# A scan's hand-written order rewoven: block 2's preparation, the first merge and the second solve in one stretch

## The chip, the cores and the metric

The kernel runs on one core of one Trainium2 chip. The metric is the device time of one execution in microseconds. Three runs of the kernel before took 2351.26, 2352.57 and 2353.73 us; the median is 2352.57.

## The reference

The reference is one layer of an encoder: a half-step feed-forward network, then a mixer made of an attention group and a recurrent group side by side, then a second half-step network. All is in float32, with 1024 tokens of width 1024. The part that matters here is the recurrent group, eight heads of width 64, scanned forwards and backwards, and the output projection of the attention group, which fills gaps in the scan:

```python
def _rwkv7_step(state, inp):
    r, w, k, v, kk, kka = inp
    sa = jnp.einsum('dbhvk,dbhk->dbhv', state, kk)
    state = state * w[..., None, :] - sa[..., :, None] * kka[..., None, :] + v[..., :, None] * k[..., None, :]
    y = jnp.einsum('dbhvk,dbhk->dbhv', state, r)
    return state, y
...
        mix = jnp.concatenate([y_att, y_rwkv], axis=-1) @ w_out[l]
        h = h + _rmsnorm(mix, mix_post_g[l])
```

## The kernel before

The kernel does not step through the tokens. It cuts them into 16 chunks of 64, takes two chunks as a block (8 blocks, both directions at once), and turns the recurrence inside a chunk into matrix products and one triangular inverse. Each block passes through these parts, written as Python generators or closures, so that the order of their pieces can be written out by hand in `scan` (lines 1068 to 1224):

- **Loads and preparation** (`prep_loads`, `prep_parts`). Per direction: `exps` (two exponentials on ScalarE), `times` (five VectorE products, lines 861 to 869, and a ScalarE copy), `triangles` (32 TensorE matmuls in two pairs of halves, `lp`, line 876, each followed by `masks`, VectorE products with a triangle mask, line 878), `turns` (32 TensorE transposes, `bp`, line 888, and two ScalarE copies). `lp` and `bp` share three PSUM banks. `store` writes the diagonal 32 x 32 blocks to DRAM, from where the solve loads them regrouped as `X`.
- **Solve** (`solve_parts`): 31 steps of two VectorE instructions each (lines 936 and 938) that invert the 32 x 32 triangles, then a transpose (line 941). `go(solve, n)` issues n steps, and each mask is followed by one.
- **Merge** (`merge_parts`): three groups of small matmuls into one PSUM bank `pa` (lines 953, 959, 966) that join the 32 x 32 inverses to 64 x 64 ones, with ScalarE copies between them (954, 961, 962, 968). It needs the block's solve.
- **Chain** (`chain_parts`): fourteen pieces: two of ScalarE copies (line 1002), and then six for each of the two chunks: `xu` (line 1014) and its copy `xs`, the old state into `st`, `xu` again (line 1027) and its copies `uv`, a first `y`, `st` and a second `y` (line 999) with the copy `yb`, and the new state `sv` (VectorE, line 1049). Chunk follows chunk through `sv`: this is the sequential spine of the scan.
- **Attended tiles** (`attended_weights`, `attended_parts`): the attention group's output projection, 8 tiles of 128 tokens. The weights are first split in high and low halves (`woh` on ScalarE, `wol` on VectorE, lines 1298 and 1299). Each tile has six pieces: transposes `yq` of the loaded rows (line 1346) and the copy `yah`; `yal` (VectorE, line 1352); four of six `po` matmuls of 512 columns each (line 1325), two for each half of the output width. The second and fourth of these copy `po` out (`yao`, line 1360), and the fourth scales the next tile's rows (line 1337). `yq` and `po` share one PSUM bank, `eo`.

The framework gives each engine its own instruction queue. `in_order` chains all instructions of the scan on TensorE, VectorE and ScalarE in the order in which `scan` emits them, so that an instruction that waits holds everything emitted after it on its engine. Loads on SyncE's queue, GpSimd's work and instructions from outside the scan are placed by the framework's scheduler. The scan's prologue handles block 0 (solved earlier) together with the end of block 1's solve and the preparation of block 2; the loop `for m in range(1, NB - 2)` runs merge and chain of block m, the solve of block m + 1 and the preparation of block m + 2; two closing passes handle blocks 6 and 7. In the trace the copies of line 961 wait for the products of line 959, which write other partitions of the same PSUM bank.

Of the kernel before, what the change touches and what calls it, by code (L numbers as in the profile page):

```python
# [10 lines left out]
F32 = mybir.dt.float32  # L11
# [10 lines left out]
H, HD = 8, 64  # L22
# [141 lines left out]
class _Kernel:  # L164
# [660 lines left out]
    def prep_loads(self, n, d, p):  # L825
# [6 lines left out]
        ak = [p.tile([128, 4, TB], F32, name=nm, tag=nm, bufs=b) for nm, b in (("ka", 2), ("kd", 1))]  # L832
        for j in range(2):
            self.load(ak[j], self.ak_d[d][4 * j:4 * j + 4, :, ls].rearrange("a p t -> p a t"))
        x3 = p.tile([128, 2, 4, TB], F32, name="in2", tag="in2", bufs=1)
        self.load(x3.rearrange("p j a t -> p (j a) t"), self.rk_d[:, :, ts].rearrange("a p t -> p a t"))
        return cum, ak, x3

    def prep_parts(self, n, p, psum, big, loaded):
# [17 lines left out]
        def times(d):  # L857
            cum, ak, x3 = loaded.pop(d)
            x = {nm: x3[:, j, :, ::-1] if d else x3[:, j] for j, nm in enumerate(("r", "kk"))}
# [83 lines left out]
    def merge_parts(self, n, blk, p, psum):  # L943
# [10 lines left out]
        A.copy(tt[:, :, 32:64], pa)  # L954
        yield
# [4 lines left out]
        for lo, hi in lohi:  # L960
            A.copy(tt[lo, :, 0:32], pa[lo])
        A.copy(am, pa)
        yield
        for j in range(NI):
            for lo, hi in lohi:
                T.matmul(pa[lo, j, :], am[hi, j, :], tt[hi, j, 32:64], start=True, stop=True)  # L966
        for lo, hi in lohi:
            A.activation(tt[lo, :, 32:64], pa[lo], AF.Copy, scale=-1.0)
# [22 lines left out]
    def chain_parts(self, n, blk, c, psum):  # L991
# [13 lines left out]
        for i in range(BLK):  # L1005
            ch = n * BLK + i
            first = ch == 0
            uv = self.chain_values(ch, c)
            sv, nx = self.states(ch, c), self.states(ch + 1, c)
# [58 lines left out]
    def scan(self, blk, NB, sp, sc, eo, pm, pp, pc, pe, homes):  # L1068
# [32 lines left out]
        loads(2, 0)  # L1101
        parts(2)
        exps, times, triangles, turns, store = P.pop(2)
        go(solve, 5)
        times(0)
        loads(2, 1)
        go(solve, 4)
        masks(triangles(0, 0), solve)
        masks(triangles(0, 1), solve)
        exps(1)  # L1110
        turns(0)
        go(solve, 3)
        times(1)
        loads(3, 0)
        masks(triangles(1, 0), solve)
        masks(triangles(1, 1), solve)
        for _ in solve:
            pass
        store()

        merge, chain, solve = begin(0)
        weights = self.attended_weights(eo, W)
        go(weights)
        go(merge)
        turns(1)
# [4 lines left out]
        solving(2)  # L1130
        go(weights)
        solve = solves.pop(2)
        rs_a = self.rstd(eo, self.ss_a.rearrange("p a b -> p (a b)"), NT * H, 1.0 / HD, EPS)
        go(chain, 6)
        go(weights)
# [584 lines left out]
```

## Time and profile before

| What | us |
|---|---|
| median of three runs | 2352.57 |
| the profiled execution, its own time | 2355.06 |
| its span | 2353.3 |
| TensorE busy | 2198.4 |
| VectorE busy | 1774.3 |
| ScalarE busy | 1025.0 |
| first merge matmul to the last stretch's end in the scan (1273.6 to 1597.5) | 323.9 |

In the profile PE is TensorE, PEld its weight loads, DVE VectorE, ACT ScalarE, POOL GpSimd and SP SyncE; a q behind a name is the engine's queue for DMA issues. A row of the timeline gives the start, the length, the engine, the line in the kernel, the operation, what it writes and reads, the shape and how many such instructions it joins; brackets at its end give the idle time before it and what ended that. A matmul's length in a row is longer than its distance to the next one, because matmuls overlap in the array. A row of stretches gives the busy time of each engine between two times, and the TensorE clock that was granted, as a share of full speed.

### The profile page before, as it was taken

The numbers are of one execution on the slowest core, as the hardware profiler recorded it, in microseconds if no ns is written. First come the engines' busy times: TensorE is split into PE (matmuls) and PEld (weight loads), VectorE is DVE, ScalarE is ACT, GpSimd is POOL, SyncE is SP. The second block draws the span as 40 slices with busy tenths as digits, with TensorE's granted clock in tenths as the row PEclk, the third lists the DMA queues.
The fourth block names the chain that finished last, engine by engine and source line by source line (L and its number), as shares of the span: only waits on it lengthen the run. The fifth ranks groups of instructions, "written<-read, shape, count | busy, mean of one in ns | idle before, by whom it ended". The sixth has DMA issues, their size and how long they took to land. (4 is left out here: it accounts for less than half of the span.)

```text
span 2353.3 us, 41391 instructions
## 1 busy us (share of the span) xinstructions
PE 2198.4 (93%) x15556; PEld 1771.9 (75%) x15556; DVE 1774.3 (75%) x2893; ACT 1025.0 (44%) x1925; POOL 538.5 (23%) x673
## 2 busy tenths in 40 slices
PE   6999999999999998999996788879889999999998
PEld 5788888788877676787774667656678888887887
DVE  7999999865675344777776666746999999997566
ACT  5333333354676404666544454445542333335453
POOL 2344344400000011322211101122024343442000
PEclk9999999999999999999986888889989999999999
DMA  5354544576652515654377454536534544448665
GB/s 150 126 177 152 171 162 151 182 256 197 224 170 100 194 46 163 186 152 144 108 186 189 118 155 139 137 121 236 173 105 165 175 155 163 169 149 269 195 190 191
DMA packets 346700, 387.74 MB, mean 165 GB/s; under 512 B 73474, under 2 KB 249346, under 8 KB 346500
## 3 DMA queue, kind: packets, MB, share of 16 engines
q1 hardware_dynamic: 294928, 271.71, 38.1%
q0 software_dynamic: 31216, 100.73, 11.5%
q10 hardware_dynamic: 20356, 12.66, 1.8%
q8 instruction: 122, 2.00, 0.4%
q14 instruction: 78, 0.64, 0.1%
HBM read 258.06 MB, written 126.94 MB: 164 GB/s over the span
## 5 line engine op out<-in xcount | busy, mean ns | idle before, releaser
L81 PE MATMUL gu<-xh,wh 128*128 128x512 f32 x704 | 276.9, 393 | 4.6 <-ACT wh L186 4.5
L186 ACT ACTIVATE wh<-raw 128x512 fp32r<-128x512 f32 (+1 forms) x273 | 168.3, 627 | 249.5 <-PE gu L81 92.8
L81 PE MATMUL gu<-xl,wh 128*128 128x512 f32 x704 | 275.6, 391 | 0.0
L81 PE MATMUL gu<-xh,wl 128*128 128x512 f32 x704 | 275.5, 391 | 0.0
L187 DVE TENSOR_TENSOR wl<-raw,wh 128x512 fp32r<-128x512 f32 (+1 forms) x273 | 269.1, 989 | 3.4 <-ACT wh L186 2.6
L421 PE MATMUL pd<-gl,gwh 128*128 128x512 f32 x616 | 241.2, 391 | 3.1 <-DVE gl L187 3.1
L421 PE MATMUL pd<-gh,gwl 128*128 128x512 f32 x616 | 240.5, 390 | 0.2 <-DVE gwl L187 0.2
L421 PE MATMUL pd<-gh,gwh 128*128 128x512 f32 x616 | 239.9, 390 | 0.4 <-DVE row L86 0.4
L86 DVE TENSOR_TENSOR row<-gu,row 128x512 f32<-128x512 f32 x308 | 206.7, 683 | 23.1 <-PE gu L81 20.8
L187 DVE TENSOR_TENSOR gwl<-graw,gwh 128x512 fp32r<-128x512 f32 (+2 forms) x187 | 119.0, 644 | 124.8 <-ACT gwh L186 122.7
L116 POOL DMA_DIRECT2D d_hid<-row x154 | 85.1, 553 | 546.8 <-DVE row L114 526.7
L186 ACT ACTIVATE gwh<-graw 128x512 fp32r<-128x512 f32 (+2 forms) x187 | 102.9, 553 | 183.5 <-PE pd L421 150.5
L81 PEld LDWEIGHTS gu<-xh,wh 128*128 128x128 f32 x704 | 133.3, 189 | 33.5 <-ACT wh L186 5.6
L81 PEld LDWEIGHTS gu<-xh,wl 128*128 128x128 f32 x704 | 133.1, 189 | 28.0 <-DVE wl L187 0.2
L81 PEld LDWEIGHTS gu<-xl,wh 128*128 128x128 f32 x704 | 133.2, 189 | 27.4
L421 PEld LDWEIGHTS pd<-gl,gwh 128*128 128x128 f32 x616 | 116.2, 189 | 28.2 <-DVE gl L187 4.4
L421 PEld LDWEIGHTS pd<-gh,gwh 128*128 128x128 f32 x616 | 115.7, 188 | 25.4 <-DVE row L86 0.7
L421 PEld LDWEIGHTS pd<-gh,gwl 128*128 128x128 f32 x616 | 116.2, 189 | 24.8 <-DVE gwl L187 0.6
L187 DVE TENSOR_TENSOR gl<-raw,gh 128x512 fp32r<-128x512 f32 x160 | 113.3, 719 | 23.6 <-ACT gh L186 23.5
L94 ACT ACTIVATE row<-row 128x512 f32<-128x512 f32 x44 | 27.8, 633 | 214.3 <-DVE row L86 214.2
L186 ACT ACTIVATE gh<-raw 128x512 fp32r<-128x512 f32 x160 | 98.1, 621 | 42.1 <-DMA raw<-in_ffn_w_down_dram 24.4
L145 POOL TENSOR_TENSOR ws<-ws 128x512 f32<-128x512 f32 x88 | 114.8, 1305 | 1.2
(364 smaller groups left out, 5214.9 us busy)
## 6 DMA issues: line engine op xcount, KB each, us to landing
d_hid<-row POOLq DMA_DIRECT2D x154, 256.0 KB, 2.4
graw<-d_hid SPq DMA_DIRECT2D x132, 256.0 KB, 3.1
raw<-in_ffn_w_gate_dram SPq DMA_DIRECT2D x88, 256.0 KB, 3.1
raw<-in_ffn_w_up_dram SPq DMA_DIRECT2D x88, 256.0 KB, 3.5
ws<-in_ffn_w_down_dram SPq DMA_DIRECT2D x88, 256.0 KB, 4.1
d_ws<-ws POOLq DMA_DIRECT2D x88, 256.0 KB, 2.3
raw<-d_ws SPq DMA_DIRECT2D x88, 256.0 KB, 2.7
raw<-in_ffn_w_down_dram SPq DMA_DIRECT2D x66, 256.0 KB, 3.6
```

The source lines that it names most:

```text
L81: self.K.nc.tensor.matmul(ps, a[:, k, :], b[:, k, :], start=(k == 0 and i == 0), stop=(k == 3 and i == 2))
L86: add = lambda o, x: V.tensor_tensor(o, ps, x, op=OP.add)
L94: A.activation(y[:, 0], y[:, 0], AF.Silu)
L116: put = lambda n, y: G.dma_start(self.hid[n - 1, j // 2], y)
L145: G.tensor_tensor(o, a, b, op=OP.subtract)
L186: self.nc.scalar.activation(h, src, AF.Copy)
L187: (eng or self.nc.vector).tensor_tensor(l, src, h, op=OP.subtract)
L421: T.matmul(ps[x], a[:, ts], b, start=(m == 0 and k == 0), stop=(m == NM - 1 and k == 2))
```

## The change

The order in `scan` is written anew, and five helpers are adapted to it.

- The prologue loads both directions of block 2 at once (the second direction's `kd` and inputs into buffers of the `eo` pool that later hold split weights), and weaves block 2's preparation, the first merge and the solve of block 1 together; the chain's pieces, the weight splits and the solve of block 2 follow in a new order, and the prologue now ends with nine pieces of attended work issued instead of six.
- In the loop, `turns(0)` moves between the chunks of the chain, and `turns(1)` behind the first merge product of the next pass (`pend`). triangles(0, 0) stands between the second and third merge products. triangles(1, 0) moves into the second chunk. Each tile's two first `po` pieces stand in two places of the pass, the two others and the next tile's transposes at its end. The extra attended tile moves from m = 3 to m = 1.
- `merge_parts` copies line 961's parts before the second group of products, and gets one more yield before its last copies.
- The raw attended weights of k = 1 and 3 are loaded into the tiles `yat` and `yal`, so that two pairs are loaded at the start.
- The second half of each `po` (dh = 1) uses the merge's PSUM bank `mg` instead of `eo`.

```diff
@@ -822,19 +823,26 @@
         with self.tc.issue_after(last):
             return product().ins
 
-    def prep_loads(self, n, d, p):
+    def prep_loads(self, n, d, p, q=None):
 
         ls = slice(n * TB, (n + 1) * TB)
         b = n if d == 0 else NC_ // BLK - 1 - n
         ts = slice(b * TB, (b + 1) * TB)
         cum = p.tile([128, 4, TB], F32, name="th_w", tag="th_w", bufs=2)
         self.load(cum, self.lr_d["w"][d][:, :, ls].rearrange("a p t -> p a t"))
-        ak = [p.tile([128, 4, TB], F32, name=nm, tag=nm, bufs=b) for nm, b in (("ka", 2), ("kd", 1))]
+        ak = [p.tile([128, 4, TB], F32, name="ka", tag="ka", bufs=2),
+              q.tile([128, 4, TB], F32, name="kd", tag="woh", bufs=8) if q else
+              p.tile([128, 4, TB], F32, name="kd", tag="kd", bufs=1)]
         for j in range(2):
             self.load(ak[j], self.ak_d[d][4 * j:4 * j + 4, :, ls].rearrange("a p t -> p a t"))
+        if q:
+            x2 = [q.tile([128, 4, TB], F32, name="in1", tag="woh", bufs=8) for j in range(2)]
+            for j in range(2):
+                self.load(x2[j], self.rk_d[4 * j:4 * j + 4, :, ts].rearrange("a p t -> p a t"))
+            return cum, ak, x2
         x3 = p.tile([128, 2, 4, TB], F32, name="in2", tag="in2", bufs=1)
         self.load(x3.rearrange("p j a t -> p (j a) t"), self.rk_d[:, :, ts].rearrange("a p t -> p a t"))
-        return cum, ak, x3
+        return cum, ak, [x3[:, j] for j in range(2)]
 
     def prep_parts(self, n, p, psum, big, loaded):
 
@@ -855,8 +863,8 @@
             A.activation(flat(cum), flat(cum), AF.Exp, scale=-1.0)
 
         def times(d):
-            cum, ak, x3 = loaded.pop(d)
-            x = {nm: x3[:, j, :, ::-1] if d else x3[:, j] for j, nm in enumerate(("r", "kk"))}
+            cum, ak, x2 = loaded.pop(d)
+            x = {nm: x2[j][:, :, ::-1] if d else x2[j] for j, nm in enumerate(("r", "kk"))}
             ei = chunks(cum)
             V.tensor_copy(gc[:, d], e4[:, :, :, C])
             pt = blk["pr"][d] = big.tile([128, 4, BLK, 128], F32, name="pr", tag=f"pr{d}")
@@ -952,18 +960,19 @@
             for r in [r for lo, hi in lohi for r in (hi, lo)]:
                 T.matmul(pa[r, j, :], D[r, j, :], self.ident[r, r], start=True, stop=True)
         A.copy(tt[:, :, 32:64], pa)
+        for lo, hi in lohi:
+            A.copy(tt[lo, :, 0:32], pa[lo])
         yield
         for j in range(NI):
             d, i, pr = j // 8, j // 4 % 2, j % 4
             for par, (lo, hi) in enumerate(lohi):
                 T.matmul(pa[hi, j, :], lm[lo, par, d, i, pr, 32:64], D[lo, j, :], start=True, stop=True)
-        for lo, hi in lohi:
-            A.copy(tt[lo, :, 0:32], pa[lo])
         A.copy(am, pa)
         yield
         for j in range(NI):
             for lo, hi in lohi:
                 T.matmul(pa[lo, j, :], am[hi, j, :], tt[hi, j, 32:64], start=True, stop=True)
+        yield
         for lo, hi in lohi:
             A.activation(tt[lo, :, 32:64], pa[lo], AF.Copy, scale=-1.0)
 
@@ -1005,8 +1014,8 @@
         for i in range(BLK):
             ch = n * BLK + i
             first = ch == 0
-            uv = self.chain_values(ch, c)
-            sv, nx = self.states(ch, c), self.states(ch + 1, c)
+            sv = self.states(ch, c)
+            uv, nx = self.chain_values(ch, c), self.states(ch + 1, c)
             bank = lambda nm: psum.tile([128, 2, 4, 64], F32, name=nm, tag=nm, bufs=1)
             xu, st, y = bank("xu"), bank("st"), bank("y")
             for d, pr, par in heads:
@@ -1099,56 +1108,64 @@
         solve = self.solve_parts(1, sp, blk[1])
         go(solve, 9)
         loads(2, 0)
+        loaded[2][1] = self.prep_loads(2, 1, sp, eo)
         parts(2)
         exps, times, triangles, turns, store = P.pop(2)
+        weights = self.attended_weights(eo, W)
+        go(weights)
         go(solve, 5)
         times(0)
-        loads(2, 1)
-        go(solve, 4)
-        masks(triangles(0, 0), solve)
-        masks(triangles(0, 1), solve)
         exps(1)
+        loads(3, 0)
+        mask = triangles(0, 0)
+        go(solve, 2)
+        masks(mask, solve)
+        mask = triangles(0, 1)
+        times(1)
+        masks(mask, solve)
         turns(0)
-        go(solve, 3)
-        times(1)
-        loads(3, 0)
-        masks(triangles(1, 0), solve)
-        masks(triangles(1, 1), solve)
-        for _ in solve:
-            pass
+        merge, chain, _ = begin(0)
+        go(merge)
+        mask = triangles(1, 0)
+        go(solve, 2)
+        masks(mask, solve)
+        go(merge)
+        mask = triangles(1, 1)
+        go(solve, 2)
+        masks(mask, solve)
         store()
-
-        merge, chain, solve = begin(0)
-        weights = self.attended_weights(eo, W)
-        go(weights)
-        go(merge)
-        turns(1)
+        solving(2)
         go(merge)
         go(chain)
         go(merge)
         go(chain)
-        solving(2)
+        for _ in solve:
+            pass
+        turns(1)
+
         go(weights)
+        go(chain, 5)
         solve = solves.pop(2)
-        rs_a = self.rstd(eo, self.ss_a.rearrange("p a b -> p (a b)"), NT * H, 1.0 / HD, EPS)
-        go(chain, 6)
-        go(weights)
-        go(solve, 4)
-        go(chain, 5)
-        go(solve, 8)
         go(weights)
         go(chain)
+        go(chain, 3)
+        go(solve, 6)
+        go(chain, 2)
+        go(weights)
+        go(solve, 6)
+        go(chain)
+        rs_a = self.rstd(eo, self.ss_a.rearrange("p a b -> p (a b)"), NT * H, 1.0 / HD, EPS)
+        go(weights)
+        rest = self.attended_parts(eo, sc, pe, pm, list(range(NT)), W, rs_a)
+        go(rest, 2)
+        parts(3)
+        go(solve, 3)
+        go(rest, 5)
         go(solve, 2)
-        rest = self.attended_parts(eo, sc, pe, list(range(NT)), W, rs_a)
-        go(weights)
-        go(rest)
-        parts(3)
-        go(rest)
-        go(solve, 3)
-        go(rest, 4)
-        go(solve, 3)
+        go(rest, 2)
         solves[2] = solve
         blk.pop(0)
+        pend = lambda: None
 
         for m in range(1, NB - 2):
             merge, chain, solve = begin(m)
@@ -1157,13 +1174,15 @@
             times(0)
             go(merge)
             loads(k, 1)
+            pend()
+            go(merge)
+            mask = triangles(0, 0)
+            go(solve, 4)
             go(merge)
             go(chain)
-            mask = triangles(0, 0)
-            go(solve, 4)
-            masks(mask, solve)
             go(merge)
             go(chain)
+            masks(mask, solve)
             masks(triangles(0, 1), solve)
             exps(1)
             go(rest)
@@ -1171,44 +1190,54 @@
             times(1)
             loads(k + 1, 0)
             go(chain, 4)
+            go(solve, 2)
+            turns(0)
+            go(chain)
             go(solve, 3)
+            go(chain, 3)
             mask = triangles(1, 0)
             go(chain)
+            masks(mask, solve)
+            go(chain)
             go(solve, 3)
-            masks(mask, solve)
-            go(chain, 5)
-            go(solve, 4)
             go(chain)
+            go(rest)
             mask = triangles(1, 1)
-            go(solve, 2)
+            go(solve, 3)
             masks(mask, solve)
             store()
             solving(k)
+            go(rest, 3)
+            go(solve, 4)
             go(rest)
-            turns(0)
-            turns(1)
-            go(solve, 2)
-            go(rest, 4)
+            if m == 1:
+                go(solve, 2)
+                go(rest, 5)
+                go(rest)
             parts(k + 1)
             for _ in solve:
                 pass
-            if m == 3:
-                go(rest, 6)
+            pend = functools.partial(turns, 1)
             blk.pop(m)
 
         merge, chain, solve = begin(NB - 2)
         go(merge)
-        go(solve, 6)
+        pend()
+        go(solve, 5)
+        go(merge)
+        go(solve, 2)
         go(merge)
         go(chain)
-        go(solve, 3)
         go(merge)
+        go(chain)
+        go(solve, 4)
         go(rest)
         go(chain)
         go(solve, 2)
-        go(chain, 5)
-        go(solve, 13)
+        go(chain, 4)
+        go(solve, 10)
         go(chain)
+        go(rest)
         go(chain, 5)
         for _ in solve:
             pass
@@ -1216,7 +1245,7 @@
         for _ in rest:
             pass
         merge, chain, solve = begin(NB - 1)
-        go(merge, 2)
+        go(merge, 3)
         go(chain)
         go(merge)
         for _ in chain:
@@ -1285,19 +1314,30 @@
 
     def attended_weights(self, p, W):
 
+        raw = {}
+
+        def load(k):
+            for dh in range(2):
+                tag = ("wor", ("yat", "yal")[dh])[k % 2]
+                raw[k, dh] = p.tile([128, 512], F32, name="wor", tag=tag, bufs=1 if k % 2 else 2)
+                self.load(raw[k, dh], self.io["w_out"][0][k * 128:(k + 1) * 128, dh * 512:(dh + 1) * 512])
+
+        load(0)
+        load(1)
+        yield
         for k in range(4):
             hl = []
             for dh in range(2):
-                r = p.tile([128, 512], F32, name="wor", tag="wor", bufs=2)
-                self.load(r, self.io["w_out"][0][k * 128:(k + 1) * 128, dh * 512:(dh + 1) * 512])
                 h = p.tile([128, 512], F32R, name="woh", tag="woh", bufs=8)
                 l = p.tile([128, 512], F32R, name="wol", tag="wol", bufs=8)
-                hl.append((h, l, r))
-            yield
-            for h, l, r in hl:
+                r = raw.pop((k, dh))
                 self.nc.scalar.activation(h, r, AF.Copy, scale=self.aog[:, k:k + 1])
                 self.nc.vector.scalar_tensor_tensor(l, r, self.aog[:, k:k + 1], h, op0=OP.mult, op1=OP.subtract)
-            W.append([(h, l) for h, l, r in hl])
+                hl.append((h, l))
+            W.append(hl)
+            if k < 2:
+                load(k + 2)
+            yield
 
     def out_weights(self, p, k0, gain=None, raw=None):
 
@@ -1324,7 +1364,7 @@
             for j, (a, w) in enumerate(((xh, h), (xh, l), (xl, h))):
                 self.nc.tensor.matmul(ps, a[:, k, ts], w, start=(k == 0 and j == 0), stop=(k == 3 and j == 2))
 
-    def attended_parts(self, p, c, psum, tiles, W, rs_a):
+    def attended_parts(self, p, c, psum, other, tiles, W, rs_a):
 
         nc, V, A, T = self.nc, self.nc.vector, self.nc.scalar, self.nc.tensor
 
@@ -1352,7 +1392,7 @@
             V.tensor_tensor(l, q, h, op=OP.subtract)
             yield
             for dh in range(2):
-                ps = psum.tile([128, 512], F32, name="po", tag="eo")
+                ps = (psum, other)[dh].tile([128, 512], F32, name="po", tag=("eo", "mg")[dh])
                 for part in range(2):
                     self.out_products(ps, W, dh, h, l, slice(0, 128), range(2 * part, 2 * part + 2))
                     if part:
```

More of the change, by code (lines that the diff above doesn't have):

```diff
@@ L1 @@
+import functools
 import math
```

## The prediction

> **What bounds the kernel now.** I read the page first, for where the time is and which engine carries it.
>
> ```profile
> span 2353.3 us, 41391 instructions
> PE 2198.4 (93%) x15556; PEld 1771.9 (75%) x15556; DVE 1774.3 (75%) x2893; ACT 1025.0 (44%) x1925; POOL 538.5 (23%) x673
> ```
>
> TensorE is busy 93% of the span, so only stretches where it waits can be shortened by an order. The change touches the scan alone. I cut the scan at the first merge matmul of each block (line 953) and asked for the busy time of each stretch.
>
> ```profile
> core 0: us, PE busy (x) PEld busy (x) DVE busy (x) ACT busy (x) POOL busy (x), PEclk, DMA share, GB/s
> 1246.30:1273.60 27.30, 13.83 (x97) 11.06 (x96) 21.02 (x55) 6.90 (x12) 7.60 (x13) 0.64 0.92 242
> 1273.60:1325.00 51.40, 29.47 (x592) 25.05 (x591) 29.44 (x82) 22.77 (x38) 5.63 (x11) 0.63 0.45 122
> 1325.00:1360.30 35.30, 31.06 (x721) 25.69 (x721) 15.42 (x35) 17.77 (x32) 5.64 (x11) 0.95 0.52 132
> 1360.30:1400.80 40.50, 33.70 (x809) 28.13 (x810) 30.80 (x89) 18.57 (x34) 5.64 (x11) 0.92 0.56 158
> 1400.80:1451.40 50.60, 42.41 (x680) 34.13 (x669) 34.59 (x101) 20.86 (x37) 5.64 (x11) 0.83 0.55 151
> 1451.40:1491.40 40.00, 34.81 (x718) 28.96 (x717) 26.03 (x75) 17.74 (x32) 5.65 (x11) 0.83 0.45 122
> 1491.40:1529.60 38.20, 32.23 (x721) 26.51 (x720) 29.89 (x86) 17.34 (x32) 4.77 (x8) 0.91 0.48 132
> 1529.60:1568.30 38.70, 27.96 (x627) 23.02 (x626) 20.88 (x69) 12.56 (x23) 9.37 (x14) 0.87 0.47 141
> 1568.30:1597.50 29.20, 24.81 (x614) 19.19 (x613) 9.78 (x16) 19.85 (x35) 4.72 (x6) 0.88 0.25 77
> ```
>
> The first two rows, the end of block 2's preparation and the pass of block 0, take 78.7 us with TensorE busy 43.3 of them at a clock of 0.63: there is most to win. The next five are the loop (m = 1 to 5; m = 3 holds an extra attended tile). In them TensorE waits 4 to 8 us each and VectorE is already busy 26 to 31 us of about 40. The last two are the two closing blocks. The chain of waits says what ends TensorE's idle time; these are from 1223 to 1598 us, as total, times, longest.
>
> ```profile
> PE yq L1346 <- DVE yat L1337: 10.0, 1, 10.0
> PE po L1325 <- DVE yal L1352: 9.5, 7, 2.3
> PE pa L959 <- issue: 8.2, 4, 3.5
> PE pa L966 <- ACT am L962: 8.0, 6, 1.9
> PE bp L888 <- DVE lm L878: 7.0, 10, 1.4
> PE po L1325 <- ACT yao L1360: 5.4, 8, 0.7
> PE pa L959 <- ACT tt L954: 5.3, 7, 0.9
> ```
>
> The waits of `bp`, `po` and `pa` are about 5 us per block, and the change names a filler or a second bank for every one of them except "issue". The question is whether VectorE lets that be kept.
>
> **Part by part: the loop, m = 2 to 5.** Rows of TensorE and then VectorE in the blocks m = 4 and 5:
>
> ```profile
> 1463.10 1.15 PE L1014 MATMUL xu<-sv,lm 128*64 128x64 f32 x32
> 1483.65 0.79 PE L1325 MATMUL po<-woh,yah 128*128 128x512 f32 x1 [1.18 <-DVE yal L1352]
> 1484.24 0.63 PE L1325 MATMUL po<-wol,yah 128*128 128x512 f32 x1
> 1490.14 0.39 PE L1325 MATMUL po<-wol,yah 128*128 128x512 f32 x1
> 1491.40 1.29 PE L953 MATMUL pa<-ident,X 32*32 32x32 f32 x128
> 1500.43 1.15 PE L1014 MATMUL xu<-sv,lm 128*64 128x64 f32 x32
> 1503.37 1.15 PE L1027 MATMUL xu<-xs,tt 64*64 64x64 f32 x32 [0.77 <-ACT xs L1017]
> 1510.92 1.10 PE L1027 MATMUL xu<-xs,tt 64*64 64x64 f32 x32
> 1529.58 1.29 PE L953 MATMUL pa<-ident,X 32*32 32x32 f32 x128
> ```
>
> ```profile
> 1472.07 0.69 DVE L878 TENSOR_TENSOR lm<-lp,k_tri 128x512 f32<-128x512 f32 x1
> 1485.89 1.07 DVE L941 STREAM_TRANSPOSE X<-Ti 128x512 f32<-128x512 f32 x1
> ```
>
> Split a block at its first chain product (`xu`). The front, 953 to `xu`, was 1451.4 to 1463.1 = 11.7 and 1491.4 to 1500.4 = 9.0 (the second with the clock full). The rest, `xu` to the next 953, was 28.3 and 29.2.
>
> The rest first. Before, the last part of VectorE's work, from the first mask of triangles(1,0) to the transpose that ends the solve, ran 1472.07 to 1486.96 = 14.9 us and started 9.0 after `xu`. It was hidden: eighteen `po` matmuls stood behind it, and 953 came 4.4 us later. In the new order triangles(1,0) stands behind the second chunk's `xu` of line 1027. By the row at 1510.92 that starts 10.5 after the block's `xu`, and takes 0.9 to the next start; turns(0) in place of a triangle before it is 0.3 longer (32 small matmuls for 16), the triangle itself takes 1.1, and the wait of 0.8 at 1503.37 belongs to that block alone: it is ready 10.5 + 0.9 + 0.3 + 1.1 − 0.8 = 12.0 after `xu`. VectorE then has the same list, one solve step more (18 for 17) and the scaling of the next attended tile, which the new order puts ahead of the transpose.
>
> ```profile
> L938 DVE TENSOR_TENSOR Ti<-Ti,ttmp 128x126 f32<-128x126 f32 (+22 forms) x124 | 31.8, 257 | 4.5
> L936 DVE TENSOR_TENSOR ttmp<-X,Ti 128x126 f32<-128x126 f32 (+22 forms) x124 | 31.3, 252 | 4.1 <-DMA X<-d_x 1.4
> L1049 DVE TENSOR_TENSOR sv<-st,gc 64x512 f32<-64x512 f32 x16 | 11.0, 687 | 3.5 <-PE st L999 3.4
> L1337 DVE TENSOR_TENSOR yat<-yat,rs 128x512 f32<-128x512 f32 x5 | 3.4, 676 | 0.0
> ```
>
> A step is 257 + 252 ns, about 0.6 with its gaps, the scaling 0.7: 14.9 + 1.3 = 16.2. So 953 can start 12.0 + 16.2 = 28.2 after `xu`, against 28.3 and 29.2 before. TensorE has done `po` and the turns by then: its last attended products end some 8 us earlier, it gets the transposes of the next tile only behind the scaling, and then waits about 5 us on the transpose of line 941 in one piece. The waits of the list above are removed and their sum comes back as this one: **VectorE becomes late next**, and the gain in this half is 0 to 1. The second bank of `po` is the merge's own: 953 has to wait for its copy as well (one ScalarE copy, 0.6), and behind 953 stands the whole front; the transposes of the next tile and the wait for line 941 cover it.
>
> The front. Line 961's copies now hold the second merge products (both copies 1.2 longer), but 32 `bp` of turns(1) fill that, and triangles(0,0) fills the wait for `am`. With rows at full clock I get 9.2, with the turn included. But TensorE comes out of a long wait, and the rows show what that does: `po` after short waits at 1483.65 was paced 0.43 (0.63 in its row) and 0.23 (0.39) once it had run on; 953 in the stretch with clock 0.63 took 1.9 for 1.2. With about 5 us of half pace the front is 9.2 + 1.4 = 10.6; its ends are 9.2 and 12.2 (half pace throughout). The Trainium skill (TensorE: Matmul & The Clock Gate, Part 1) says that the clock halves after an idle window of about 3.4 us and comes back after as long a busy one; by it the front would be 9.2 + 1.7 = 10.9, 1.2 us more over four blocks. The trace agrees on the size, not on the condition: `po` at 1483.65 ran at half pace with no gap before it above 1.2 us.
>
> With 0.9 for instruction waits ("issue" is 8.2 us over four places in the list) a block is 10.6 + 28.2 + 0.9 = 39.7. Four blocks are 158.8; before, 40.5 + 50.6 + 40.0 + 38.2 = 169.3. So −10.5, nearly all of it the extra tile that leaves m = 3. The load of `X` behind the later masks(1,1) I cost at nothing: VectorE meets it after 2.5 us of products of times(0), and waits there for triangles(0,0) anyway; with that cover gone it is 1 to 2 per block.
>
> **m = 1** gets that tile. Its solve is more than half done, so VectorE is light (15.4 busy before) and TensorE sets the pace: front 9.1, chain 15.4 (12.0 as above and three groups of 32 at about 1.1, as `xu` in its rows), then `po` 1.4, triangle 1.1, `po` 2.8, turn 0.6, a wait of 1.5 for `yal`, `po` 5.5, turn 0.6, together 38.0; with 1.5 for clock and instruction waits 39.5, before 35.3: +4.2.
>
> **m = 6** loses half a tile, among it the `yq` and its wait. Front 10.6, first chunk to the state product behind 23 solve steps about 7, second chunk 6.3, `po` 2.8 and its copy 0.7: 27.4; with 3 for instruction waits (3.5 before, at 959) 30.5 against 38.7: −8.2. **m = 7** only moves a yield: 0. The sv/uv swap: 0.
>
> **The start.** Rows of the pass of block 0: the load of the attended rows, the landing line of the eight such loads, and TensorE.
>
> ```profile
> 1264.08 0.33 SPq L182 DMA_DIRECT2D yat<-d_ya  x1
> DMA to landing us min/median/max: 2.5/4.6/9.9
> 1303.89 1.15 PE L999 MATMUL y<-lm,uv 128*64 128x64 f32 x31
> 1315.00 1.11 PE L1346 MATMUL yq<-ident,yat 128*128 128x128 f32 x4 [9.96 <-DVE yat L1337]
> 1317.58 0.79 PE L1325 MATMUL po<-woh,yah 128*128 128x512 f32 x1 [1.47 <-DVE yal L1352]
> 1325.00 1.29 PE L953 MATMUL pa<-ident,X 32*32 32x32 f32 x128
> ```
>
> Loads of block 2's second direction go into `eo`, so they no longer wait for times(0), and with four loads of raw weights they pass loads(3, 0) on SyncE's queue, which has until 1310. Merge 0 starts about 1266 instead of 1273.6, and VectorE ends solve 1 at about the same time as before. The lead of 7 us is then mostly given back: the weight splits are now queued on ScalarE and VectorE ahead of each state product. The second pair stands ahead of chunk 0's (4 us of TensorE idle), the third pair and six solve steps ahead of chunk 1's. The last `y` of block 0 ends about 1299 instead of 1305.0, its state product about 1306. The last pair's raw weights lie in the tile of the attended rows, so the first rows load only after it: at 1308, with at least 2.5 to land, where before the load went out at 1264. Scale, `yq`, `yah`, `yal` follow, and `po` starts about 1314.5 instead of 1317.58. Then 24 matmuls, about half of them slow, and a turn: 953 at 1322.8 instead of 1325.0, with six `po` more done. So −2.2; ends −10 (the rows' load is hidden) and +6 (the `eo` loads land late and times(1), now ahead of masks(0,1), holds VectorE and with it turns(0) and merge 0).
>
> **Sum**: −2.2 + 4.2 − 10.5 − 8.2 = −16.7. The profiled execution took 2355.06 (span 2353.3 and 1.8 around it), the median of three runs is 2352.57, 2.5 lower; the sum is taken off both. Forecast: 2338.4 profiled, **2335.9** median. 0.2% is 4.7 us, about what can be told from no change.
>
> **Rivals.** *Slower: the cold clock.* The 5 us wait at the block's end leaves TensorE at half pace not for the front alone but through the first chunk: front 12.2, and 4 more to triangles(1,0). A block is then 12.2 + 16.0 + 16.2 + 0.9 = 45.3, and four are 22.4 above my sum: 2358. It decides from 43.9 per block, where 4 x 4.2 eats the 16.7. For it: the clock of 0.63 in the two first stretches. Against it: in the blocks before, half pace ended after 4 to 7 us of work. 0.13.
>
> *More: VectorE is not late.* Its work per block is 31 steps of 0.6, eight masks, ten products of times, four sv, two tile operations and a transpose, about 33 in all. If masks and steps fit between, a block nears 35 and the total is 4 x 4.7 lower: 2317. For it: the waits listed; against it: VectorE's order is fixed, and 14.9 of it stands behind one triangle. 0.14.
>
> *No change: the start costs.* The `eo` loads, the split pairs and the late first rows make the start +10 instead of −2.2: 2348, and with a bad m = 6 about 2352. 0.15. That leaves 0.58 for the forecast.
>
> **How the numbers follow.** The forecast's own unknowns (start −10 to +6, front 9.2 to 12.2 in four blocks, m = 6 by 3) give about 2323 to 2347. Reaching to the rivals until a fifth is left out: 2318 to 2353. Faster by over 0.2% is below 2347.9: 0.53 of the forecast's 0.58, the 0.14, and a little of the third: 0.70. Within 0.2%: 0.15; slower: 0.15.
>
> **What would show it.** Right: line 941's transposes end just ahead of each 953 in m = 2 to 5, a TensorE wait of 4 to 6 us stands there, `po` waits on `yao` are gone, blocks last 38 to 41; 953 of block 1 comes at 1320 to 1326; m = 6 is about 30. Wrong: no such wait and blocks of 35; blocks above 43.9 with a clock under 0.8; or the first `po` of the scan after 1320.

## The result, and the profile after

The changed kernel took 2368.5 us (median of 4 runs, 2365.8 to 2370.1) against 2351.9 for the kernel before beside it: ratio 1.0069, 95% interval 1.0052 to 1.0086. It is slower by 17 us, where 16.7 less was forecast. Page of after:

```profile
span 2367.4 us, 41414 instructions
PE 2192.9 (93%) x15556; PEld 1772.7 (75%) x15556; DVE 1771.2 (75%) x2893; ACT 1023.0 (43%) x1925; POOL 541.6 (23%) x673
```

The work is the same to the instruction on every engine; what grew is waiting. The stretches of after, cut at the first merge product of each block (line 961 there; lines of after stand up to 40 later), with the columns of the prediction's table:

```profile
1277.20:1332.50 55.30, 32.26 (x637) 27.37 (x637) 29.16 (x83) 23.58 (x40) 6.12 (x11) 0.69 0.28 80
1332.50:1376.60 44.10, 38.31 (x728) 32.43 (x728) 22.80 (x55) 17.78 (x32) 5.63 (x11) 0.88 0.55 151
1376.60:1420.60 44.00, 33.16 (x717) 28.09 (x719) 30.75 (x90) 20.20 (x36) 4.80 (x9) 0.84 0.49 133
1420.60:1462.40 41.80, 31.59 (x720) 26.79 (x723) 29.80 (x88) 18.35 (x33) 6.59 (x12) 0.87 0.51 141
1462.40:1503.20 40.80, 33.23 (x716) 28.61 (x717) 29.71 (x88) 18.35 (x33) 6.51 (x12) 0.79 0.55 156
1503.20:1546.70 43.50, 34.22 (x716) 29.08 (x716) 29.67 (x86) 17.09 (x31) 6.52 (x11) 0.77 0.37 106
1546.70:1578.40 31.70, 26.72 (x632) 22.52 (x632) 19.67 (x67) 12.94 (x24) 6.62 (x11) 0.84 0.42 129
1578.40:1610.80 32.40, 24.61 (x605) 19.77 (x605) 8.11 (x12) 17.69 (x31) 6.21 (x7) 0.74 0.29 93
```

| stretch | before | predicted | after | miss |
|---|---|---|---|---|
| first merge product of block 1, at | 1325.0 | 1322.8 | 1332.5 | +9.7 |
| m = 1 | 35.3 | 39.5 | 44.1 | +4.6 |
| m = 2 to 5 | 169.3 | 158.8 | 170.1 | +11.3 |
| m = 6 | 38.7 | 30.5 | 31.7 | +1.2 |
| m = 7 | 29.2 | 29.2 | 32.4 | +3.2 |

The scan ends at 1610.8 instead of 1597.5, 13.3 later; the span grew by 14.1. From the list of waits of after, 1223 to 1612 us, rows of TensorE and VectorE (total, times, longest):

```profile
PE pa L961 <- issue: 21.3, 5, 4.9
PE yq L1386 <- DVE yat L1377: 13.1, 1, 13.1
DVE pr L875 <- DMA in<-d_rk: 12.8, 1, 12.8
DVE ttmp L944 <- DMA X<-d_x: 12.5, 3, 4.6
PE pa L969 <- ACT tt L964: 11.5, 7, 3.5
PE yq L1386 <- issue: 7.5, 4, 1.9
```

The waits of `po` for `yao` are gone. In their place stand one of 4.9 us before each merge of blocks 3 to 6 (the fifth entry of the first row, 1.7, is a stop inside block 5's first products), one for the first attended rows, and 12.8 us of VectorE for a load. That load, in the rows of SyncE, VectorE and TensorE:

```profile
1259.03 2.76 SPq L645 DMA_DIRECT2D d_vt<-vts  x4
1262.40 0.54 SPq L183 DMA_DIRECT2D in<-d_rk  x1
1263.61 1.99 SPq L183 DMA_DIRECT2D in<-d_rk  x2
1273.63 0.69 DVE L875 TENSOR_TENSOR pr<-in,e 128x512 f32<-128x512 f32 x1 [12.84 <-DMA in<-d_rk]
1276.18 1.11 PE L896 MATMUL bp<-ident,bk 64*128 64x64 f32 x15 [14.01 <-DVE lm L886]
```

The pair at 1263.61 is block 2's r and kk in `eo`. On SyncE's queue it stands behind the stores of `vts` and behind block 3's inputs (1262.40), and lands about 1273.6. VectorE stands for 12.8 us, TensorE for 14. Of VectorE's wait some 3 us pass before the pair is issued; the rest is its landing, 9.3 us from the issue.

The end of m = 2 and the front of m = 3, in rows of VectorE, SyncE and TensorE:

```profile
1419.45 1.04 DVE L949 STREAM_TRANSPOSE X<-Ti 128x512 f32<-128x512 f32 x1
1426.76 0.19 DVE L944 TENSOR_TENSOR ttmp<-X,Ti 128x31 f32<-128x31 f32 x1 [3.82 <-DMA X<-d_x]
1421.16 0.38 SPq L183 DMA_DIRECT2D ka<-d_ak  x1
1421.72 1.50 SPq L183 DMA_DIRECT2D X<-d_x  x1
1415.07 0.63 PE L1386 MATMUL yq<-ident,yat 128*128 128x128 f32 x4 [1.87 <-issue]
1420.59 1.93 PE L961 MATMUL pa<-ident,X 32*32 32x32 f32 x128 [4.89 <-issue]
1426.50 1.13 PE L974 MATMUL pa<-tt,am 32*32 32x32 f32 x58
1430.20 0.31 PE L974 MATMUL pa<-tt,am 32*32 32x32 f32 x6 [2.58 <-issue]
1430.44 2.05 PE L884 MATMUL lp<-pr,bk 64*128 64x128 f32 x16
1434.70 1.15 PE L1023 MATMUL xu<-sv,lm 128*64 128x64 f32 x32
```

"issue" before 961 is the transpose: it ends at 1420.49, 961 starts at 1420.59. The front, 961 to `xu`, is 14.1 us. `X`, whose masks were done 8 us earlier, is issued behind a `ka` that waits for VectorE. At m = 2 ScalarE holds the front (rows of ScalarE and TensorE):

```profile
1379.71 0.61 ACT L874 COPY bk<-bk 64x512 f32<-64x512 f32 x1 [0.76 <-DVE bk L873]
1380.35 0.58 ACT L962 COPY tt<-pa 128x512 f32<-128x512 f32 x1
1380.83 1.16 ACT L964 COPY tt<-pa 32x512 f32<-32x512 f32 x2
1382.05 1.48 PE L969 MATMUL pa<-X,lm 32*32 32x32 f32 x64 [3.48 <-ACT tt L964]
```

The copies of `tt` are queued behind the copy of `bk`, which waits for VectorE; VectorE is late because it stood 6.4 us for `yah` before the previous tile's `yal`.

### The profile page after: what moved, and what is told of

It reads as the page before. It is cut to its first block, busy times and chain, and to the rows that moved or that the text cites. A ratio compares the mean times of both kernels' runs of the same rounds, so it can differ in the third digit from the quotient of the medians.

```text
span 2367.4 us, 41414 instructions
## 1 busy us (share of the span) xinstructions
PE 2192.9 (93%) x15556; PEld 1772.7 (75%) x15556; DVE 1771.2 (75%) x2893; ACT 1023.0 (43%) x1925; POOL 541.6 (23%) x673
## 3 DMA queue, kind: packets, MB, share of 16 engines
q0 software_dynamic: 31216, 100.73, 11.3%
## 4 chain that ended last, share of the span: by engine, by line
PE 39%; DVE 6%; issue 3%; ACT 3%; DMA 2%; SPq 0%; ACTq 0%; POOL 0%; DVEq 0%; POOLq 0%
PE gu L82 18%; PE pd L422 9%; PE po L1365 2%; PE lp L884 2%; PE st L1008 1%; PE zr L524 1%; PE pw L1365 1%; DVE Ti L946 1%; DVE ttmp L944 1%; PE xu L1023 1%; PE xu L1036 1%; PE y L1008 1%; PE pa L969 1%; DVE lm L886 1%; PE pa L974 0%
```

## The experiments

Times are medians; the interval is that of the ratio to the kernel before on the same chip. From each trace: when block 1's first merge product starts, and the loop from there to the last `y`.

| run | us | ratio, 95% | block 1 at | loop |
|---|---|---|---|---|
| before | 2351.9 | | 1325.0 | 272.5 |
| after | 2368.5 | 1.0052–1.0086 | 1332.5 | 278.3 |
| s0_start_before | 2361.0 | 1.0016–1.0053 | 1327.0 | 281.7 |
| l0_loop_before | 2361.1 | 1.0026–1.0063 | 1338.2 | 269.6 |
| s1_third_loads_later | 2370.6 | 1.0066–1.0099 | 1334.7 | 272.6 |
| s2_loads_on_pool | 2366.1 | 1.0045–1.0086 | 1327.3 | 279.6 |
| f1_warm | 2374.0 | 1.0061–1.0122 | 1331.4 | 278.0 |
| f2_merge_first | 2364.9 | 1.0036–1.0076 | 1334.9 | 272.4 |
| f3_x_first | 2368.0 | 1.0035–1.0073 | 1334.4 | 272.4 |
| g1_solve_early | 2368.9 | 1.0042–1.0080 | 1334.4 | 271.6 |
| g2_copies_and_order | 2370.5 | 1.0044–1.0090 | 1338.8 | 278.0 |
| g3_all_mended | 2352.4 | 0.9980–1.0009 | 1328.4 | 273.9 |
| h1_tile_at_3 | 2369.5 | 1.0054–1.0095 | 1331.4 | 278.1 |
| h2_turns_back | 2369.6 | 1.0064–1.0094 | 1330.6 | 279.3 |
| f5_warm_front | 2366.2 | 1.0039–1.0077 | 1336.3 | 274.5 |
| p0_two_banks | 2344.1 | 0.9955–0.9980 | 1325.2 | 263.2 |
| p1_banks_merge_first | 2337.5 | 0.9908–0.9959 | 1320.2 | 261.1 |
| p2_rows_early | 2335.2 | 0.9915–0.9956 | 1314.5 | 267.4 |

Read the last two columns with care: after, s0, s1 and s2 share one loop, and it took 272.6 to 281.7 in their four traces. A difference of 5 us in one trace is not told; waits and paces in the rows are. And s0, l0, f5 and g3 were profiled in executions 5 to 7 us above their medians, so their traces do not stand for those medians to within that.

**Start and loop apart.** s0 has before's start (and its weights) with after's loop, l0 the reverse.

> The start (everything up to block 1's first merge product) as before the change, the loop, merge and attended order as after it. In the two traces the start is 8.5 us longer after the change (7.5 later on the clock, with the scan entered 1 us earlier) and the loop from block 1 on 5.8 us longer (278.3 against 272.5). Theory A, the two losses are separate: about 2369 - 8.5 = 2360 us, with block 1's first merge product near 1325. Rival B, the new start buys the loop something (block 2's turns done, one attended tile ahead), so that the old start makes the loop longer: 2364 or more. Rival C, the loss is all the start's and the loop's 5.8 us are its after-effect: 2352 to 2355.

> The start as after the change, cut to the attended steps that the old loop expects, and the loop, the merge and the attended order as before it. Theory A: 2352 + 8 = 2360 us, with VectorE's 12.8 us wait for block 2's reversed r and kk still there. Rival B: above 2364. Rival C, the loss is all the start's: 2366 to 2370.

(s0's start does three attended steps more than before's, l0's three fewer than after's, as their loops expect.) They lost 9.4 and 9.5 us (2361.02 and 2361.09 against 2351.6), together 18.9, about after's 16.6; by the intervals 3.8 to 12.5 and 6.1 to 14.8. Theory A stands; it is not all the start's.

**The late load.**

In short form:

```diff
 s1:  exps(1)
-     loads(3, 0)
      ...
      times(1)
+     loads(3, 0)
 s2, in prep_loads(2, 1), for kd and both in1:
-     self.nc.sync.dma_start(...)
+     self.nc.gpsimd.dma_start(...)
```

> After, with block 3's first loads emitted behind block 2's second times, so that they no longer stand on SyncE's queue ahead of block 2's r and kk. Theory Q, the 12.8 us wait is a queue of transfers (1.25 MB of block 3's and block 2's inputs and 1 MB of weights within 5 us): r and kk are issued about 1.5 us earlier and land 3 to 5 us earlier, and the time falls by as much, to 2364 or 2365. Theory M, the memory of those tiles comes free late, or SyncE stands behind the stores of vts until 1261.8 us: they land no more than 1.5 us earlier, and the time stays within 2 us of 2368.5.

s1 tells nothing of the load: SyncE still issued block 3's inputs first (its order is not the emission's; only TensorE, VectorE and ScalarE are pinned to that), and the wait was 13.5.

> After, with block 2's second kd and its two r/kk tiles issued from GpSimd's queue and not from SyncE's, where moving the emission of block 3's loads had not changed the order. Theory M (SyncE holds them behind the stores of vts, which are issued until 1261.8 us, and then behind block 3's loads): GpSimd issues them behind its memsets, about 1253 to 1257, they land by 1263, VectorE's wait falls from 12.8 to under 3 us, merge 0 starts near 1267 and block 1's first merge product near 1324: 2369 - 8.5 = 2360. Rival, their memory itself comes free only at about 1261, whatever queue asks: the wait stays above 8 us and the time above 2365.

In s2 GpSimd issues them at once, and merge 0 starts 12.6 us earlier (rows of GpSimd, then TensorE):

```profile
1251.77 0.76 POOL L183 DMA_DIRECT2D kd<-d_ak  x1
1252.52 1.50 POOL L183 DMA_DIRECT2D in<-d_rk  x2
1264.66 1.55 PE L961 MATMUL pa<-ident,X 32*32 32x32 f32 x100
1316.03 1.11 PE L1386 MATMUL yq<-ident,yat 128*128 128x128 f32 x4 [13.04 <-DVE yat L1377]
1327.29 1.29 PE L961 MATMUL pa<-ident,X 32*32 32x32 f32 x128 [0.24 <-ACT yao L1400]
```

The pair lands 6.0 us after its issue, before VectorE needs it. So the memory was free by then and the late issue from SyncE's queue was the cause. But block 1 starts only 5.2 us earlier, since the wait of 13 us for the first attended rows stays; the time misses the theory's 2360.

**The front: clock, ScalarE, X, turns.** f1 adds `warm(22)` products in the tail; f5 adds `warm(20)` there, 3 behind the first merge step, 2 behind the second; `warm` multiplies `woh` by itself into the idle `y` bank. The edits in short form:

```diff
 f1, f5:  go(rest)
+         warm(n)
 f2:      -times(0)
          go(merge)
         +times(0)
 f3: +add_manual_dep(ka's load, X's load)
 h2: -pend = functools.partial(turns, 1)
     +turns(1)      # behind go(rest, 3)
```

> After, with 22 more products per pass of blocks 1 to 5 (into chain's y bank, read by nobody): 6 before the next tile's transposes and 16 behind them, so that TensorE is busy at full width while VectorE finishes the solve. At 0.228 us each they take 5 us, the two waits there 6.8. Theory, the front of the next block (from the first merge product to the first xu, 13 to 16 us) runs at half pace because TensorE stood still before it: the front falls to 10.6 to 12.2 us in blocks 2 to 6, 2 us or more each, and the time to 2355 to 2360. Rival, the front is slow for its own sparse work and for waits on ScalarE: it stays above 13 us, and the time at 2366 to 2372.

> After, with products that nobody reads: 20 in the wait in front of the next merge, 3 behind its first step and 2 behind its second (0.23 us each at full pace). f1_warm took the half pace from the first products of the front only; it came back behind the next waits. Theory, the merge's own 32-wide products and its waits do not hold the clock and a few full-width ones among them do: what is left of half pace in the fronts of blocks 3 to 6 (18 us in after, 12 in f1_warm) falls below 5, against some 5 us of added products and 2 to 3 of the tail's overrun: 2362 to 2368. Rival: the half pace stays, and the time is 2374 or more.

f1's row behind the filler and f5's front at m = 4:

```profile
1420.42 1.29 PE L961 MATMUL pa<-ident,X 32*32 32x32 f32 x128
1430.08 0.79 PE L1373 MATMUL po<-woh,yah 128*128 128x512 f32 x1
```

```profile
1470.40 1.27 PE L961 MATMUL pa<-ident,X 32*32 32x32 f32 x126
1476.31 1.16 PE L884 MATMUL lp<-pr,bk 64*128 64x128 f32 x16
1481.63 1.15 PE L1023 MATMUL xu<-sv,lm 128*64 128x64 f32 x32
```

All 22 came behind the transposes. With the tail filled, 961 ran at full pace before every block of the loop (1.29; in after 1.93 at m = 3, 4 and 6), but half pace was back by `po` (0.79 where a full one has 0.50), and fronts stayed at 12.5 to 15.5 us: f1 as a whole misses, and on the time so does the rival. In f5 the fronts of m = 4 and 5 were 11.2 and 11.4 instead of 13.5 and 16.2, at a granted clock of 1.00 in both, and these blocks 38.6 and 38.8, below the forecast's 39.7; in m = 2 and 3 they were 16.4 and 15.6 all the same. So a front at full pace is 2 to 5 us shorter. That the fillers held the clock there is likely and not shown: without any, f2's front of m = 2 came to 10.1 (clock 1.00) and f3's of m = 4 to 9.7 (0.84). The mean granted clock of the profiled executions is 0.961 in f1 and f5, as in before (after 0.953), but the fillers take time themselves, and f5's time falls by no more than can be told (2366.2). No run joins them with f2's order.

> After, with the first merge step emitted ahead of times(0), so that ScalarE's three copies to tt stand ahead of its copy of bk, which waits for VectorE. Theory: the 3.5 us waits of the second merge products for tt in blocks 1 and 2 (and the 3.6 us ones put down to issue) fall to 1.5 or less: 4 to 9 us in all, 2360 to 2365. Rival: bk's copy and with it the turns behind the first merge step come as much later; within 2 us of 2368.5.

The waits of 3.5 fell to 2.1 and 2.0; the front of m = 2 from 15.5 to 10.1, of m = 1 to 13.1, but that of m = 3 rose from 14.1 to 16.0. The time is at the upper end of the theory's range, and its interval overlaps after's.

> After, with the load of X ahead of the next block's ka on SyncE's queue. ka waits there for VectorE's bk at the start of the next pass, and X, whose stores are out 6 us earlier, behind it. Theory: X arrives 5 us earlier, VectorE's waits for it (4.6, 4.0 and 3.8 us) go, and the last transpose of the solve, for which TensorE waits 4.9 us in front of five merges, comes up to 3 us earlier: 2355 to 2362. Rival: the slow front has covered the X wait; within 2 us of 2368.5.

The waits for `X` fell from 12.5 to 4.6 us in all, and VectorE's waits for the triangles rose from 31.8 to 35.6: the slow front had covered them. The rival holds.

> After, with turns(1) at the end of its own pass, where TensorE then waits for VectorE, and not behind the next block's first merge step. Theory, TensorE's work in the wait is free and work in the front is not: the fronts get 0.7 us shorter at full pace and up to 1.4 at half pace, and the copies to bt no longer stand between ScalarE's copies for the merge: 3 to 8 us, 2361 to 2365. Rival: within 2 us of 2368.5.

A miss: the work left the front, the waits for `tt` there grew (0.7 to 1.8 at m = 4), and the time did not move: the rival holds.

**VectorE's run, and everything mended.** g1 is f3 with `go(solve, 8)` for `go(solve, 4)` in the front and none behind `go(rest, 3)`. g2 is f2 with the line 964 copies again behind the second products. g3 joins s2, f2, f3, g1 and g2, with the odd raw weights in `yah` and `yal`.

> After, with X ahead of ka on SyncE (as in f3_x_first) and four more steps of the solve done in the front of the pass, where VectorE waits 3.4 us for the triangles, in place of the four behind the third attended part. Theory, VectorE's run from the front's masks to the last transpose (27.4 us in every block) sets the length of blocks 2 to 5: four steps of some 0.5 us less in it, so 1.5 to 2 us less of the 4.9 us wait in front of five merges, 7 to 10 us in all from 2368: 2358 to 2361. Rival, TensorE or the clock sets it: within 3 us of 2368.

From `xu` to the next 961 took 26.3 to 26.7 us in m = 2 to 5 instead of 27.4 to 28.4, and the wait before the merges fell from 4.9 to 4.3, so VectorE's run does set that half; the fronts stayed at 14.2 to 15.7 and the time did not fall. On the time the rival holds.

> After, with ScalarE's order in the merge as before the change (the two half copies to tt behind the second products) and with the first merge step emitted ahead of times(0). Theory, the front is long because TensorE waits in it for ScalarE's copies and then runs at half pace: its waits for tt fall to 1 us and below, the fronts of blocks 1 to 6 from 13.5 to 16 us to 9 to 11 in most blocks, and the time by 10 us or more, to 2358 or less. Rival, the copies only change places, and what f2_merge_first gave (3.6 us) is all: 2363 to 2367.

A miss of both: the fronts stayed at 12.8 to 15.8, and the time is above the rival's.

> After with all of it: block 2's second inputs on GpSimd's queue, the odd weights in yah's and yal's buffers so that the first attended rows load early, X ahead of ka, ScalarE's copies and the first merge step in the other order, four solve steps early. Theory, the change's order is sound where its side effects are taken away: the single gains (3 + 3.5 + 0.5 + about 8 + the start's 13 us wait for the rows cut by 3) add to about 17 us, 2351, at the level of the kernel before. Rival, the gains overlap: 2357 to 2362.

At the level of before, with an interval apart from after's. The profiled executions of after and g3 are 10.3 us apart, and 8.5 of these lie in the scan (end at 1602.3): 4.1 in the start, where the wait for the first attended rows fell from 13.1 to 11.0, and 4.1 in m = 2 to 5. The fronts are no shorter there (13.5 to 15.9 us, granted clock 0.50 to 0.70), so g3's gain is not theirs. The single mendings do not add up to 16, and the other buffers for the raw weights were tried in no run alone; what makes up the rest stays open.

**The tile.** `if m == 1` becomes `if m == 3`.

> After, with the extra attended tile behind block 3 as before the change and not behind block 1. Theory, the tile costs the same wherever TensorE has to do it between a full VectorE run and the next merge: block 1 falls from 44 to 35 or 36 us, block 3 rises from 42 to 50 or 51, the time within 3 us of 2368.5. Rival, what the prediction took (4.2 us at block 1 against 10.6 at block 3): 2374 or more.

Block 1 fell by 9.7 to 34.4, block 3 rose by 6.2 to 48.0, blocks 2 and 4 by 2.1 and 1.3: the four together 170.6 against 170.7. The tile costs the same in either place.

**One part alone, on the kernel before.** p0 takes the two banks (`ps = (other, psum)[dh]`), p1 also f2's order, p2 also the first tile ahead of eight solve steps.

> The kernel before with one part of the change alone: the attended products of the two halves in two banks (the first half on the merge's bank, since here the second half's two parts lie on both sides of the merge). Theory: the seven waits of po for the copy yao, 4.7 us in the trace of before, go, and the blocks in which TensorE runs to the next merge without another wait get shorter: 2348 to 2350 us. Rival: what ends the wait before the next block is VectorE's last transpose or the next X, and the time stays at 2352.

> The kernel before with the two banks for the attended products and the first merge step ahead of times(0). Theory, the tt copy behind bk's costs 8.2 us of waits in seven blocks there: 2 to 5 us below the two banks alone (2344), 2339 to 2342. Rival: the copy of bk then holds the triangles as long: 2343 to 2346.

> The kernel before with two banks and the first merge step ahead of times(0) (2337.5), and with the first attended tile's scaling, transposes and first half ahead of eight of block 2's solve steps in the start. Theory, TensorE's 10 us wait there before the change (13 after it) is VectorE's order, the scaling standing behind those steps and the last weights: block 1's first merge product comes 4 to 6 us earlier and the time falls to 2331 to 2334. Rival, the solve's steps are then missing later and VectorE is late in block 1: 2336 to 2340.

p0 has no wait of `po` for `yao`, and is faster than before beyond doubt: this part of the change is worth 7.5 us where TensorE ends the blocks. That is more than the 4.7 us of waits that the expectation counted; no run separates the rest. p1 and p2 are told apart from before as well; that p1 beats p0 is not shown, since the intervals touch and p1's start, which the edit doesn't touch, came 5 us earlier too. In p2 block 1 starts 5.7 us earlier than in p1, and its triangles then wait for VectorE:

```profile
1314.51 1.29 PE L953 MATMUL pa<-ident,X 32*32 32x32 f32 x128
1321.27 2.08 PE L876 MATMUL lp<-pr,bk 64*128 64x128 f32 x16 [3.53 <-DVE bk L869]
```

Its loop is 6.3 longer, the time no different. Both sides of the expectation held: the 10 us wait is VectorE's order, and VectorE has no slack to pay for it.

## Why the prediction was wrong, step by step

**The start, −2.2 forecast, +7.5 measured: the sign failed.** The step was "they pass loads(3, 0) on SyncE's queue". They did not: I read the emission as the queue's order. The text named this end, "the `eo` loads land late and times(1) ... holds VectorE", and priced it at +6. With the load early (s2) merge 0 started at 1264.7, as forecast (1266). The second half failed by itself. The pass of block 0 was mis-sized: in s2 its last `y` ended at 1303.0, forecast 1299, the rows' load went out at 1312.7, forecast 1308, and `po` came at 1318.6, forecast 1314.5. In that pass VectorE stood 7.6 and 7.2 us for the second and third pair's `woh`, which ScalarE takes behind the chain's copies, and the rows' scaling comes behind the third pair, six solve steps, the state product and the last pair. That other orders on VectorE remove the wait is shown on the kernel before alone (p2).

**The front, 10.6 forecast, 13.5 to 16.2 measured in m = 2 to 5, and 9.1 against 13.8 in m = 1: the term that was mis-sized.** Its products need 7.7 us at full pace (1.2 for 961, 0.65 `bp`, 1.1 each for 969, 974 and two `lp`, 1.4 for six `po`). The rest of the mean 14.8 is 2.5 of waits and 4.6 of half pace; I had 1.5 and 1.4. The granted clock of the four fronts was 0.70, 0.77, 0.54 and 0.50 (before 0.92, 0.72, 0.71 and 1.00). The trace of before could have warned: the half pace at `po` of 1483.65, on which the prediction's "about 5 us" and its "agrees on the size" rest, lasted from 1482.64 to 1489.47, 6.83 us. The five fronts are 21.6 us above forecast, 18 when the 0.9 per block that the sum kept for instruction waits is set against them: 18 of the miss of 30. Two of the waits I had not seen at all: `tt` behind `bk`'s copy on ScalarE (3.5 in m = 1 and 2).

**The rest of a block, 28.2 forecast, 27.4 to 28.4 measured: right, with its reason.** The transpose ends just ahead of each merge, TensorE waits 4.9 us for it; in m = 1 the rest came out at 30.4, as forecast. VectorE became late next, so the waits that the change fills came back as one.

**The extra tile** was forecast at −10.5 in m = 2 to 5 and +4.2 in m = 1. Moving it back changes nothing (h1). The saving in m = 3 was real (51.3 to 41.8) and went to m = 1 and into the slow fronts. (The prediction's table cuts blocks 2 and 3 at 1400.80, but line 953 began at 1400.02; their sum is the same. And its "26 to 31" for VectorE holds for three of the five loop blocks: m = 1 has 15.4, m = 3 34.6.)

**X at nothing: right** (f3). **m = 6: right**, 31.7. **m = 7, forecast 0:** line 964's copies also hold its second products (1.7 for 0.7), and a wait of 3.6 inside them without a releaser stands where before had 1.6.

**The rivals.** "The cold clock" said half pace through the whole front, and was right in m = 4 and 5 (clock 0.54 and 0.50); it did not go on into the chunks, so blocks are 42.5 and not 45.3. "The start costs" came true at +7.5, where it said +10. With the sizes measured, the start alone would have left a gain of 7 (16.7 − 9.7) and the fronts alone no change (18). I gave them chances as if one excluded the other, but they sit in different places and add up: that made the range too narrow above.

## What to carry to other kernels

An order pinned on three engines says nothing of the fourth's queue: read the load's place there before calling it early, and issue an urgent load from a queue with nothing ahead of it. When an order takes waits from TensorE, ask which engine is late next; if it is one as full as VectorE here, the waits come back in one piece, and a wait in one piece can cost the clock as well. Parts of a reordering can be worth more alone: the second bank gave 7.5 us by itself, while the whole change lost 17.

## What the runs showed of the hardware

The clock fell late and came back late. At m = 1 of after, TensorE was at full pace, waited 3.50 us, and then:

```profile
1337.26 1.20 PE L969 MATMUL pa<-X,lm 32*32 32x32 f32 x64 [3.50 <-ACT tt L964]
1338.39 2.08 PE L884 MATMUL lp<-pr,bk 64*128 64x128 f32 x16
1344.25 0.79 PE L1365 MATMUL po<-woh,yah 128*128 128x512 f32 x1
1345.24 0.40 PE L1365 MATMUL po<-woh,yal 128*128 128x512 f32 x1
```

Half pace began about 1.1 us after the restart and ended at 1345.2, 6.8 us later. The granted clock in the traces shows why these times: it is either 0.50 or 1.00, and in all 18 traces it changes only at whole steps of 3.41 us. Stretches of after cut at such steps (columns as in the tables of stretches):

```profile
1334.94:1338.35 3.41, 1.09 (x64) 1.09 (x64) 3.24 (x9) 2.23 (x4) 0.00 (x0) 1.00 0.66 194
1338.35:1341.76 3.41, 3.41 (x76) 3.15 (x70) 1.95 (x7) 1.82 (x3) 0.00 (x0) 0.50 0.93 257
1341.76:1345.18 3.42, 3.42 (x40) 3.03 (x35) 1.79 (x5) 2.69 (x5) 0.00 (x0) 0.50 0.02 2
1369.07:1372.48 3.41, 3.41 (x10) 2.64 (x9) 0.69 (x1) 0.00 (x0) 0.00 (x0) 0.50 0.69 220
1382.72:1392.96 10.24, 10.24 (x150) 8.63 (x144) 6.13 (x19) 5.85 (x10) 0.00 (x0) 0.50 0.32 92
```

In the first step TensorE worked 1.09 us, and the clock was halved from its end. In the second it was busy without a gap, with the merge's 32-wide products and `lp`, and the clock stayed at half; it was full again behind the third, which ends in `po`. The fourth holds nothing but 128x512 products, and one such step was enough. The last row is the front of m = 2: three steps without a gap, and full clock only behind the one that `po` and `xu` fill. So in these places a busy step of the merge's products did not bring the clock back. Whether their width decides that, no run tried.

The Trainium skill (TensorE: Matmul & The Clock Gate, Part 1) gives a free-running window of about 3.4 us for both changes. The traces agree on the window (3.41 us); one busy window was not always enough here.

In blocks 6 and 7 of every kernel TensorE stopped for 0.6 to 4.8 us in the middle of a group of merge products with no releaser in the trace; in after it also did so in m = 3 (2.6) and m = 5 (1.7). No run tried what that is.
